# A hybrid decoder layer on one core: inputs handed over a second time with channels on rows, and the first pair of heads issued earlier

## The chip, the core and the metric

The kernel runs on one core of a Trainium2 chip. The metric is device time in microseconds (us) of one execution, as the median of several runs. A core has five engines with instruction queues of their own: TensorE (PE, matmuls; its weight loads are shown apart as PEld), VectorE (DVE), ScalarE (ACT), GpSimd (POOL) and SyncE (SP), which issues most of the transfers here. SP's transfers and POOL's transfers are moved by the same 16 DMA engines.

## What is computed

The input `x` has 256 tokens of 2048 channels, in fp32. The layer is a SwiGLU block of width 5632, a mixer, a second SwiGLU block, and a last norm:

```
x = x + 0.5 * (silu(n1(x) @ w1) * (n1(x) @ w3)) @ w2          # ffn1
h = rms_norm(x, mix_norm);  p = h @ w_in                      # q|k, v, o, gates, u
y = [ mLSTM heads (4 heads, causal, 64-token chunks) | S5 (64 groups, complex diagonal scan) ] @ w_out
x = x + y
x = x + 0.5 * swiglu_2(rms_norm(x));   out = rms_norm(x, final_norm)
```

In a head the 256x256 scores of q and k are multiplied by a decay matrix and then multiplied with v. In S5, each group has a state of 64 complex numbers; its output is the real part of the states times `c_re + i c_im`.

## The kernel before

**Precision by three products.** Each fp32 operand is split in two parts (`xh`, `xl` and `whi`, `wlo`), and a product is `xh*whi + xl*whi + xh*wlo`. A weight step is 256 rows by 512 columns (512 KB): SP loads it into `wraw` (L155), ACT casts it to `whi` (L157), DVE subtracts to get `wlo` (L159), and PE runs 12 matmuls of 128x512 (`step_tok`, L177). There are four buffers each of `wraw`, `whi` and `wlo`, and `weights` keeps up to three further steps in preparation (`AHEAD`).

**The activations need channels on rows.** `x` comes with tokens on rows. `transpose_x` (L341) turns a chunk of 512 channels with 8 PE transposes, ACT writes `xh` times the norm's gain (L346), DVE writes `xl` (L351). The gains are themselves loaded as rows and turned by PE (`vec0` at L272 and `vecs` at L294).

**The opening** is the function `start`: the first product of ffn1 (8 steps), in an order written out by hand for PE, ACT and DVE. It loads x chunk by chunk, transposes a chunk after steps 0, 2 and 4, runs `self.warm` (matmuls on a zero tile, L312) before the data is there, and takes the squares for the norm (`sumsq`) in steps 4 to 7. SP's order is written out by hand in the whole kernel. Elsewhere the order on PE, ACT, DVE and POOL is set when the kernel is built, out of program order and readiness; each engine then takes its instructions one after the other.

**Hooks and background tasks.** `self.after(n, f)` runs `f` after n further weight steps; `self.bg` is a list of small tasks of which `tick` issues a few after each step (the S5 parameters during ffn1, and the S5 scan of eight groups `j` during the mixer: load, drive, scan, unrotate, emit, act). For each `j`, `per_j` builds the S5 matrices; its `stage_c` and `trans` spread C over two parities of groups with a mask (DVE), turn it with two PE transposes (L734) and copy it out of PSUM (ACT L735, L736).

**The mixer around the change.** The products come in the order u, o, q|k, v, then `w_out`. The v product has two halves `c` of 8 steps each, here called v0 and v1. Its result is moved out by ACT into `vx[c]` (L1040). During v1 the hooks run: `scores(0)` after step 1, `scores(1)` after 2, `heads(0)` after 4, `scores(2)` after 5, `scores(3)` after 6, `heads_T(0)` after 7. `scores(h)` is four PE matmuls (L964, L965) and one DVE instruction that writes `Dm` (L966). `heads(0)` is 12 PE matmuls that read `Dm` of heads 0 and 1 and `vx[0]`, and take all four banks of the PSUM pool `tp` (L991, L994); ACT and DVE evacuate them. `heads_T(0)` turns the result (L1024), ACT writes `hmh` (L1029), DVE writes `hml` (L1030), and the first `w_out` product reads both. On the DVE queue between them stand the weights' subtractions, the S5 scan (L867) and the S5 output `yT` (L894); on ACT's stand the weights' casts and the S5 activation (L898), which reads `yT`.

Of the kernel before, what the change touches and what calls it, by code (L numbers as in the profile page):

```python
# [8 lines left out]
F32 = mybir.dt.float32  # L9
# [7 lines left out]
P = 128  # L17
S = 256
# [22 lines left out]
WARM = 8  # L41
MORE_WARM = 4
# [20 lines left out]
class _Layer:  # L63
# [87 lines left out]
    def fetch(self, name, k, kk, c0, n):  # L151
        nc = self.nc
        view = self.wview(name)
        raw = self.wraw.tile([P, KK * NC], F32, name="wraw")[:, :kk * n]
        nc.sync.dma_start(out=raw.rearrange("p (k n) -> p k n", n=n), in_=view[:, k:k + kk, c0:c0 + n])  # L155
        hi = self.whi.tile([P, KK * NC], F32R, name="whi")[:, :kk * n]
        nc.scalar.copy(hi, raw)  # L157
        lo = self.wlo.tile([P, KK * NC], F32R, name="wlo")[:, :kk * n]
        nc.vector.tensor_sub(lo, raw, hi.bitcast(F32))  # L159
        return hi.rearrange("p (k n) -> p k n", n=n), lo.rearrange("p (k n) -> p k n", n=n)  # L160
# [28 lines left out]
    def start(self, acc, view, gain):  # L189

        W = lambda i: self.weights(view, i * KK, KK, 0, NC)
        M = lambda i, w: self.step_tok(acc, self.xs, [(i * KK, 0), (i * KK + 1, 0)], w, NC, i == 0, i == 7)
        T = lambda c, halves=(0, 1): self.transpose_x(c, gain, halves)
# [44 lines left out]
    def setup(self):  # L238
# [16 lines left out]
        vec0 = self.s5p.tile([KD, P], F32, name="vec0", tag="s5k0")  # L255
        nc.sync.dma_start(out=vec0, in_=self.a["ffn1_norm"][0].rearrange("(k p) -> k p", p=P))
# [13 lines left out]
        self.cols0 = c.tile([P, KD], F32, name="cols0")  # L270
        b = self.bank()
        nc.tensor.transpose(b[:, :KD], vec0, self.ident[:KD, :KD])  # L272
        nc.vector.tensor_copy(self.cols0, b[:, :KD])
        rows = 16 + 16 + 32 + 8 * 4
        vecs = self.s5p.tile([rows, P], F32, name="vecs", tag="s5k0")
        r = 0
        where = {}
        for name, n in (("mix_norm", 16), ("ffn2_norm", 16), ("conv_w", 32), ("conv_b", 8), ("mlstm_norm", 8),
                        ("d_skip", 8), ("b_glu", 8)):
            src = self.a[name][0]  # L280
            if name == "conv_w":
                src = src.rearrange("w (j p) -> (w j) p", p=P)
            elif name == "d_skip":
                src = src.rearrange("(j r) h -> j (r h)", r=8)
            else:
                src = src.rearrange("(k p) -> k p", p=P)
            nc.gpsimd.dma_start(out=vecs[r:r + n, :], in_=src)
            where[name] = r
            r += n
        self.cols = c.tile([P, rows], F32, name="cols")  # L290

        def late():
            b = self.bank()
            nc.tensor.transpose(b[:, :rows], vecs, self.ident[:rows, :rows])  # L294
            nc.vector.tensor_copy(self.cols, b[:, :rows])
            w = where["b_glu"]
            nc.vector.tensor_scalar(self.cols[:, w:w + 8], self.cols[:, w:w + 8], 0.5, None, op0=ALU.mult)
            w = where["mlstm_norm"]
            nc.vector.tensor_scalar(self.cols[:, w:w + 8], self.cols[:, w:w + 8], 0.5, None, op0=ALU.mult)
# [3 lines left out]
        nc.vector.memset(self.gcol, 0.0)  # L303
        for i, name in enumerate(("b_i", "b_f")):
            nc.gpsimd.dma_start(out=self.gcol[32 * i:32 * i + H, :], in_=self.a[name][0].rearrange("(h o) -> h o", o=1))
# [62 lines left out]
    def ffn(self, l, chunk_done):  # L368
        nc = self.nc
        w1, w3, w2 = (f"ffn{l}_{n}" for n in ("w1", "w3", "w2"))  # L370
        with ExitStack() as ctx:
# [4 lines left out]
            for hi_, n in enumerate(HALVES):  # L376
                gs = []
                self.rate = self.ffn1_rate if l == 1 else 1
                for c in range(n):
                    cc = c0 + c  # L380
                    ks = [(k, k) for k in range(KD)]
                    p1 = self.pair()
                    if l == 1 and cc == 0:
                        self.start(p1, w1, lambda k: self.cols0[:, k:k + 1])
                    else:
                        self.gemm_tok(p1, self.xs, w1, ks, cc * NC, NC)
                    s = []
                    for t in range(TT):
                        s.append(fp.tile([P, NC], F32, name=f"s{t}"))
                        nc.scalar.activation(s[t], p1[t], AF.Silu, scale=self.rstd[:, t:t + 1])  # L390
# [117 lines left out]
    def s5_params(self, ctx):  # L508
# [13 lines left out]
        craw = [sp.tile([P, NJ, 64], F32, name=f"craw{i}") for i in range(2)]  # L522
# [14 lines left out]
        for i, nm in enumerate(("c_re", "c_im")):  # L537
            load(out=craw[i], in_=self.a[nm][0].rearrange("(j r) h p -> (r h) j p", r=8))
# [4 lines left out]
        maskg = sp.tile([P, 2], F32, name="maskg")  # L543
        maskq = sp.tile([P, 4], F32, name="maskq")

        def layout():
# [11 lines left out]
            V.tensor_reduce(maskg, self.ident.rearrange("p (q g h) -> p g q h", q=4, g=2), op=ALU.add, axis=AX.XY)  # L558
# [130 lines left out]
        def per_j(j):  # L689
# [26 lines left out]
            stc = [st.tile([P, 2, 64], F32, name=f"stc{ri}") for ri in range(2)]  # L716
# [61 lines left out]
    def mixer(self, chunk_done):  # L778
# [4 lines left out]
        with ExitStack() as ctx:  # L783
# [453 lines left out]
```

## Time and profile before

| what | value |
|---|---|
| time, median of 3 runs | 1839.52 us (1839.28 to 1840.48) |
| the profiled execution: its own time | 1839.91 us |
| its span, first to last instruction | 1838.2 us |
| mean granted TensorE clock | 0.996 |
| busy: PE, DVE, ACT, POOL | 99%, 58%, 45%, 19% |
| transfers | 358.26 MB, mean 195 GB/s |

The profiled execution's time is its span and 1.7 us around it. Busy is the time in which an engine had an instruction running; matmuls are pipelined and their ends are modelled, so PE's 99% says that it had almost always something to do, not that it ran at its peak. An "idle" in brackets behind a row is the time for which the engine had nothing to do before it, and the instruction that ended this.

### The profile page before, as it was taken

To read this page: it belongs to the slowest core of one execution; us is meant where nothing else is said; L and a number is where in the kernel's file an instruction comes from. 1 tells how busy PE (TensorE), PEld (TensorE's weight loads), DVE (VectorE), ACT (ScalarE), POOL (GpSimd) and SP (SyncE) were. 2 spreads that over 40 slices of the span, in tenths; PEclk is the share of its full clock that TensorE was granted. 3 is DMA by queue.
4 is the path that set the end of the run, shared out by engine and by line. 5 is a ranking of instruction groups with operands and counts; after the bars stand their busy time and mean duration, and the time that the engine had idled before them with its cause. 6 is when DMAs were issued, how large, how long until landed. Compare 5 with 4: busy or idle time off the path is not lost.

```text
span 1838.2 us, 24018 instructions
## 1 busy us (share of the span) xinstructions
PE 1821.5 (99%) x9174; PEld 1527.0 (83%) x9174; DVE 1064.4 (58%) x1261; ACT 818.1 (45%) x982; POOL 348.9 (19%) x519
## 2 busy tenths in 40 slices
PE   9999999999999999999999999999999999999998
PEld 7888888888888888998977988888888888888887
DVE  5546855555555555578888665454544545454554
ACT  6444444334444445444454564444443334444343
POOL 4000799920000000065545100000000000000011
PEclk9999999999999999999999999999999999999999
DMA  8666676676666665767784556666665666666563
GB/s 275 196 186 185 192 217 214 213 242 196 196 197 195 188 198 195 198 181 208 184 211 149 190 189 201 193 192 189 189 187 192 193 194 191 189 193 186 193 193 128
DMA packets 185652, 358.26 MB, mean 195 GB/s; under 512 B 12064, under 2 KB 18336, under 8 KB 185408
## 3 DMA queue, kind: packets, MB, share of 16 engines
q1 hardware_dynamic: 181344, 344.51, 63.1%
q0 software_dynamic: 4048, 11.16, 1.7%
q8 instruction: 72, 1.18, 0.3%
q10 hardware_dynamic: 144, 1.05, 0.1%
q14 instruction: 44, 0.36, 0.1%
HBM read 344.61 MB, written 11.01 MB: 193 GB/s over the span
## 4 chain that ended last, share of the span: by engine, by line
PE 95%; DVE 2%; DMA 2%; issue 1%; ACT 0%; ACTq 0%; POOLq 0%; POOL 0%; SPq 0%; DVEq 0%
PE accb L177 84%; PE accb L225 2%; PE accb L231 2%; PE accb L226 2%; DVE wlo L159 1%; PE tpb L492 1%; DMA wraw<-in_w_in_dram 1%; PE tpb L341 0%; DMA wraw<-in_ffn_w_dram 0%; PE tpb L852 0%; PE accb L482 0%; PE accb L481 0%; PE accb L480 0%; PE tpb L891 0%; PE tpb L928 0%
## 5 line engine op out<-in xcount | busy, mean ns | idle before, releaser
L159 DVE TENSOR_TENSOR wlo<-wraw,whi 128x1024 fp32r<-128x1024 f32 x622 | 791.1, 1274 | 677.4 <-ACT whi L157 676.8
L157 ACT CAST whi<-wraw 128x1024 fp32r<-128x1024 f32 x622 | 654.4, 1053 | 885.3 <-PE accb L177 814.4
L177 PE MATMUL accb<-whi,xh 128*128 128x512 f32 x1536 | 603.5, 393 | 0.6 <-ACT whi L157 0.6
L177 PE MATMUL accb<-whi,xl 128*128 128x512 f32 x1536 | 598.9, 390 | 0.8 <-DVE xl L351 0.8
L177 PE MATMUL accb<-wlo,xh 128*128 128x512 f32 x1536 | 410.7, 389 | 0.0
L177 PEld LDWEIGHTS accb<-whi,xh 128*128 128x128 f32 x1536 | 289.0, 188 | 61.6 <-ACT whi L157 1.3
L177 PEld LDWEIGHTS accb<-whi,xl 128*128 128x128 f32 x1536 | 289.0, 188 | 60.3 <-DVE xl L351 1.6
L177 PEld LDWEIGHTS accb<-wlo,xh 128*128 128x128 f32 x1536 | 288.3, 188 | 60.1
L177 PE MATMUL accb<-whi,gh 128*128 128x512 f32 x664 | 259.8, 391 | 0.0
L177 PE MATMUL accb<-whi,gl 128*128 128x512 f32 x664 | 258.4, 389 | 0.0
L177 PE MATMUL accb<-wlo,gh 128*128 128x512 f32 x664 | 177.5, 389 | 0.0
L177 PEld LDWEIGHTS accb<-wlo,gh 128*128 128x128 f32 x664 | 124.6, 188 | 25.9
L177 PEld LDWEIGHTS accb<-whi,gh 128*128 128x128 f32 x664 | 124.6, 188 | 25.6
L177 PEld LDWEIGHTS accb<-whi,gl 128*128 128x128 f32 x664 | 124.7, 188 | 25.5
L1201 POOL TENSOR_TENSOR x<-x,fn 128x512 f32<-128x512 f32 x6 | 12.1, 2041 | 689.9 <-ACT junk L323 689.9
L703 POOL TENSOR_TENSOR tr<-s5rot,sp 128x128 f32<-128x128 f32 (+6 forms) x112 | 55.5, 496 | 160.2 <-DVE sp L643 156.7
L225 PE MATMUL accb<-xh,whi 128*128 128x256 f32 x256 | 63.5, 286 | 0.0
L226 PE MATMUL accb<-xl,whi 128*128 128x256 f32 x256 | 62.8, 283 | 0.0
L705 POOL TENSOR_TENSOR s5rot<-tr,tr 128x128 f32<-128x128 f32 (+6 forms) x112 | 61.0, 557 | 3.3
L704 POOL TENSOR_TENSOR tr<-s5rot,sp 128x128 f32<-128x128 f32 (+6 forms) x112 | 57.2, 511 | 0.0
L764 POOL DMA_DIRECT2D spillw<-s5w x16 | 8.6, 541 | 249.6 <-ACT s5w L735 239.2
L225 PEld LDWEIGHTS accb<-xh,whi 128*128 128x128 f32 x256 | 49.1, 192 | 0.8 <-issue 0.4
(316 smaller groups left out, 1345.5 us busy)
## 6 DMA issues: line engine op xcount, KB each, us to landing
wraw<-in_ffn_w_dram SPq DMA_DIRECT2D x528, 512.0 KB, 3.8
wraw<-in_w_in_dram SPq DMA_DIRECT2D x64, 512.0 KB, 5.7
wraw<-in_w_out_dram SPq DMA_DIRECT2D x32, 512.0 KB, 4.2
spillrot<-s5rot POOLq DMA_DIRECT2D x8, 512.0 KB, 5.4
spillw<-s5w POOLq DMA_DIRECT2D x16, 256.0 KB, 4.6
s5rot<-spillrot SPq DMA_DIRECT2D x8, 512.0 KB, 6.9
s5w<-spillw SPq DMA_DIRECT2D x16, 256.0 KB, 7.1
wraw<-in_w_glu_dram SPq DMA_DIRECT2D x8, 512.0 KB, 3.7
```

The source lines that it names most:

```text
L157: nc.scalar.copy(hi, raw)
L159: nc.vector.tensor_sub(lo, raw, hi.bitcast(F32))
L177: nc.tensor.matmul(acc[t][:, :n], lhsT=x, rhs=wt, start=first and t not in seen, stop=last and t not in left)
L225: nc.tensor.matmul(o(nt), lhsT=wh[:, kk, ns(nt)], rhs=xh, start=st, stop=False, **kw)
L226: nc.tensor.matmul(o(nt), lhsT=wh[:, kk, ns(nt)], rhs=xl, start=False, stop=False, **kw)
L231: nc.tensor.matmul(o(nt), lhsT=wl[:, kk, ns(nt)], rhs=xh, start=False, stop=sp, **kw)
L492: nc.tensor.transpose(b[:, o:o + P], s[t][:, kt * P:(kt + 1) * P], self.ident)
L703: G.tensor_tensor(tr[0][:, :, :k], rv[:, 0, :, 0:k], u0, op=ALU.mult)
L704: G.tensor_tensor(tr[1][:, :, :k], rv[:, 1, :, 0:k], u1, op=ALU.mult)
L705: G.tensor_tensor(rv[:, a, :, k:2 * k], tr[0][:, :, :k], tr[1][:, :, :k], op=op)
L764: nc.gpsimd.dma_start(out=d, in_=t)
L1201: nc.gpsimd.tensor_tensor(self.x[c][:, t, :], self.x[c][:, t, :], self.fn[:, c * NC:(c + 1) * NC], op=ALU.mult)
```

## The change

It has four parts.

1. **x with channels on rows.** A copy of x with channels on rows (`xT`) is handed over beside x. In the opening SP loads `xT` in place of x (the first chunk in two halves, the first weight step in two halves too); ACT and DVE write `xh` and `xl` from it, and the PE transposes of the opening go. Splits of x and of weights are written two steps ahead of the matmuls. x itself is still wanted for the norm and the sum: it is loaded in steps 4 to 7, its squares are taken in steps 1 to 4 of the next product (`w3`), and `finish_rstd` and the silu of the first product follow there. The zero-tile matmuls are 9 in place of 8 and 4. The raw `xT` lies in the `gl` buffers, which are free then.
2. **Channel vectors** come as one array `cols`, loaded first by SP (57 KB in rows of 448 bytes); two PE transposes, their copies, seven loads on POOL's queue and one on SP's go. The gate biases are one load on POOL's queue in place of two.
3. **S5's C** is handed over turned and spread (`cT`). Per `j`, two loads of 64 KB on POOL's queue write it into the tile `w2`; two PE transposes, two DVE products and two ACT copies go, and one ACT instruction, which changes the sign of the imaginary part in place, is added. Two loads of C on POOL's queue before that (256 KB each) go.
4. **Order in the v product.** `scores(0)` and `scores(1)` run after steps 6 and 7 of v0, `heads(0)` after step 2 of v1, `scores(2)` and `scores(3)` after steps 4 and 5, `heads_T(0)` after step 6.

```diff
-WARM = 8
-MORE_WARM = 4
+WARM = 9
...
         with self.tc.manual_schedule(engines={ET.PE, ET.Activation, ET.DVE}):
-            self.load_x(0)
-            T(0, (0,))
-            self.ahead.append((self.steps[0], self.fetch(*self.steps.pop(0))))
-            T(0, (1,))
-            self.warm(MORE_WARM)
-            self.ahead.append((self.steps[0], self.fetch(*self.steps.pop(0))))
-            self.load_x(1)
+            load_xT(0, 0, 2)
+            load(0, KK)
+            load_xT(0, 2, 4)
+            load(1)
+            prepare(0)
+            load_xT(1)
+            load(2)
+            prepare(1)
+            load_xT(2)
+            load(3)
             for i in range(8):
-                M(i, W(i))
-                if i % 2 == 0 and i < 6:
-                    T(i // 2 + 1)
-                if i % 2 == 0 and i < 4:
-                    self.load_x(i // 2 + 2)
+                prepare(i + 2)
+                if i == 0:
+                    load_xT(3)
+                if i + 4 < 10:
+                    load(i + 4)
                 if i >= 4:
-                    self.sumsq(i - 4)
-        self.finish_rstd()
+                    self.load_x(i - 4)
+                self.step_tok(acc, self.xs, [(i * KK, 0), (i * KK + 1, 0)], ready.pop(0)[1], NC, i == 0, i == 7)
+        self.ahead = ready
...
+        def split_x(k):
+            c, i = divmod(k, 4)
+            g = self.col("ffn1_norm", k)
+            nc.scalar.activation(self.xh[c][:, i, :], raw[c][:, i, :], AF.Copy, scale=g)
+            nc.vector.scalar_tensor_tensor(self.xl[c][:, i, :], raw[c][:, i, :], g, self.xh[c][:, i, :].bitcast(F32),
+                                           op0=ALU.mult, op1=ALU.subtract)
...
                     if l == 1 and cc == 0:
-                        self.start(p1, w1, lambda k: self.cols0[:, k:k + 1])
+                        self.start(p1, gp)
+                        for i in range(4):
+                            self.after(1 + i, lambda i=i: self.sumsq(i))
+                        self.after(4, self.finish_rstd)
+                        self.after(4, silu)
...
             def stage_c():
                 for ri in range(2):
-                    src = craw[ri][:, j, :].unsqueeze(1).broadcast_to([P, 2, 64])
-                    self.tc.keep_in_program_order(V.tensor_tensor(
-                        stc[ri], src, maskg.unsqueeze(2).broadcast_to([P, 2, 64]), op=ALU.mult))
+                    nc.gpsimd.dma_start(out=w2[:, ri * P:(ri + 1) * P], in_=self.a["cT"][ri, :, j, :])
...
-                b2 = self.bank()
-                for ri in range(2):
-                    nc.tensor.transpose(b2[:, ri * P:(ri + 1) * P], stc[ri].rearrange("p g q -> p (g q)"), self.ident)
-                nc.scalar.copy(w2[:, 0:128], b2[:, 0:128])
-                nc.scalar.activation(w2[:, 128:256], b2[:, 128:256], AF.Copy, scale=-1.0)
+                nc.scalar.activation(w2[:, 128:256], w2[:, 128:256], AF.Copy, scale=-1.0)
...
+                if c == 0:
+                    self.after(6, lambda: scores(0))
+                    self.after(7, lambda: scores(1))
                 acc = self.pair()
                 self.gemm_tok(acc, self.xs, win, ks, V0 + c * NC, NC)
...
                 if c == 0:
-                    for h, n in enumerate((1, 2, 5, 6)):
-                        self.after(n, lambda h=h: scores(h))
-                    self.after(4, lambda: heads(0))
-                    self.after(7, lambda: heads_T(0))
+                    self.after(2, lambda: heads(0))
+                    self.after(4, lambda: scores(2))
+                    self.after(5, lambda: scores(3))
+                    self.after(6, lambda: heads_T(0))
```

## Rows read from the trace of the kernel before

**Rows 1.** The page, part 1: busy us, share of the span, instructions, by engine.

```profile
PE 1821.5 (99%) x9174; PEld 1527.0 (83%) x9174; DVE 1064.4 (58%) x1261; ACT 818.1 (45%) x982; POOL 348.9 (19%) x519
```

**Rows 2.** Chain that ended last, around the opening: start us, us, what.

```profile
25.75 0.87 PE tpb L341 x8
26.62 24.50 PE accb L177 x108
```

**Rows 3.** Timeline of PE, opening: start us, us, line, out<-in, [idle before <-releaser].

```profile
1.52 3.59 PE L312 MATMUL tpb<-junk 128*128 128x512 bf16 x8 [1.52 <-DVE junk L260]
5.97 1.09 PE L341 MATMUL tpb<-ident,x 128*128 128x128 f32 x8 [0.69 <-DMA x<-in_x_dram]
8.49 0.50 PE L177 MATMUL accb<-whi,xh 128*128 128x512 f32 x1 [0.57 <-ACT whi L157]
...
34.63 0.39 PE L177 MATMUL accb<-whi,xh 128*128 128x512 f32 x1
```

**Rows 4.** Windows of the opening: busy us by engine, PEclk, DMA share, GB/s last.

```profile
8.50:12.50 4.00, 4.00 (x22) 3.41 (x23) 3.16 (x5) 2.67 (x4) 3.54 (x5) 1.00 1.06 402
12.50:17.50 5.00, 4.96 (x22) 3.79 (x21) 3.98 (x6) 2.52 (x5) 0.00 (x0) 1.00 1.06 264
```

**Rows 5.** Timeline, opening: POOL's first load in small pieces; ACT's third weight cast.

```profile
8.39 1.22 POOL L526 DMA_DIRECT2D wgr<-in_w_in_dram  x1 [1.51 <-DMA vecs<-in_ffn_norm_dram]
...
11.38 1.04 ACT L157 CAST whi<-wraw 128x1024 fp32r<-128x1024 f32 x1 [1.26 <-DMA wraw<-in_ffn_w_dram]
```

**Rows 6.** Groups by line on ACT, first 60 us: count, busy us, mean ns.

```profile
L346 ACT ACTIVATE xh<-tpb,cols 128x256 fp32r<-128x256 f32 x16 | 6.4, 474 | 4.6 <-PE tpb L341 4.6
```

**Rows 7.** Loads: queue, count, KB each, median us from issue to landing.

```profile
vec<-in_ffn_norm_dram SPq DMA_DIRECT2D x1, 8.0 KB, 1.6
...
vecs<-in_conv_b_dram POOLq DMA_DIRECT2D x1, 4.0 KB, 5.8
```

**Rows 8.** Chain that ended last, around one `trans` of ffn1.

```profile
241.43 13.62 PE accb L177 x60
255.70 19.08 PE accb L177 x84
```

**Rows 9.** Timeline of PE in v1 and at the start of `w_out`.

```profile
940.62 0.59 PE L964 MATMUL tpb<-qkc 128*128 128x256 f32 x2
...
952.92 1.10 PE L991 MATMUL tpb<-vx,Dm 128*128 128x257 f32 x4 [2.57 <-DVE Dm L966]
...
968.64 1.03 PE L1024 MATMUL tpb<-ident,oth 128*128 128x128 f32 x8
...
973.57 0.50 PE L177 MATMUL accb<-whi,hmh 128*128 128x512 f32 x1
976.29 0.50 PE L177 MATMUL accb<-whi,hml 128*128 128x512 f32 x1 [2.22 <-DVE hml L1030]
```

**Rows 10.** Windows of 20 us around v1 and `w_out`; PEclk is third from last.

```profile
940.00:960.00 20.00, 17.43 (x72) 13.71 (x70) 15.51 (x14) 8.61 (x16) 10.99 (x6) 0.91 0.81 226
960.00:980.00 20.00, 17.54 (x115) 13.92 (x115) 17.12 (x31) 9.16 (x18) 11.60 (x7) 0.95 0.39 122
980.00:1000.00 20.00, 20.00 (x97) 15.74 (x96) 14.67 (x29) 11.88 (x25) 4.16 (x4) 0.97 0.55 186
```

**Rows 11.** Timeline of DVE in the same stretch.

```profile
940.59 4.46 DVE L159 TENSOR_TENSOR wlo<-wraw,whi 128x1024 fp32r<-128x1024 f32 x2
944.98 0.47 DVE L894 SCALAR_TENSOR_TENSOR yT<-uT,cols,tpb 128x256 f32<-128x256 f32 x1
...
970.28 3.42 DVE L867 TENSOR_TENSOR_SCAN A<-Rt,A 128x512 f32<-128x512 f32 x2 [0.71 <-POOL A L860]
...
975.76 0.87 DVE L1030 SCALAR_TENSOR_TENSOR hml<-tpb,cols,hmh 128x256 fp32r<-128x256 f32 x2
```

**Rows 12.** Timeline of ACT in the same stretch.

```profile
945.48 0.42 ACT L898 ACTIVATE yT<-yT 128x256 f32<-128x256 f32 x1 [6.70 <-DVE yT L894]
...
946.74 1.26 ACT L1040 ACTIVATE vx<-accb,rstd 128x512 f32<-128x512 f32 x2
```

More of the change, by code (lines that the diff above doesn't have):

```diff
@@ L149, in weights, with fetch, load, split_tiles @@
         return w
-    def fetch(self, name, k, kk, c0, n):
-        nc = self.nc
[L153 to L160, printed above, removed]
+    def fetch(self, *step):
+        return self.split(self.load(*step))
+    def load(self, name, k, kk, c0, n, parts=1):
+        raw = self.wraw.tile([P, KK * NC], F32, name="wraw")[:, :kk * n].rearrange("p (k n) -> p k n", n=n)
+        m = kk // parts
+        for i in range(0, kk, m):
+            self.nc.sync.dma_start(out=raw[:, i:i + m, :], in_=self.wview(name)[:, k + i:k + i + m, c0:c0 + n])
+        return raw
+    def split_tiles(self):
+        return (self.whi.tile([P, KK * NC], F32R, name="whi"), self.wlo.tile([P, KK * NC], F32R, name="wlo"))
+    def split(self, raw, tiles=None, ks=None):
+        nc = self.nc
+        kk, n = raw.shape[1:]
+        hi, lo = (t[:, :kk * n].rearrange("p (k n) -> p k n", n=n) for t in tiles or self.split_tiles())
+        ks = ks or slice(0, kk)
+        nc.scalar.copy(hi[:, ks, :], raw[:, ks, :])
+        nc.vector.tensor_sub(lo[:, ks, :], raw[:, ks, :], hi[:, ks, :].bitcast(F32))
+        return hi, lo
     def step_tok(self, acc, xs, part, w, n, first, last):
@@ L254, in setup @@
         xin = self.a["x"][0].rearrange("(t p) n -> p t n", p=P)
-        vec0 = self.s5p.tile([KD, P], F32, name="vec0", tag="s5k0")
-        nc.sync.dma_start(out=vec0, in_=self.a["ffn1_norm"][0].rearrange("(k p) -> k p", p=P))
+        rows = sum(n for _, n in _COLS)
+        self.cols = c.tile([P, rows], F32, name="cols")
+        nc.sync.dma_start(out=self.cols, in_=self.a["cols"])
         self.load_x = lambda i, a=0, b=NC: nc.sync.dma_start(out=self.x[i][:, :, a:b],
@@ L269, in setup @@
         nc.vector.memset(self.mhalf, -0.5)
[L270 to L287, printed above, removed]
+        where, r = {}, 0
+        for name, n in _COLS:
             where[name] = r
             r += n
-        self.cols = c.tile([P, rows], F32, name="cols")
         def late():
[L293 to L299, printed above, removed]
+            for name in ("b_glu", "mlstm_norm"):
+                w = where[name]
+                nc.vector.tensor_scalar(self.cols[:, w:w + 8], self.cols[:, w:w + 8], 0.5, None, op0=ALU.mult)
         self.after(6, late)
@@ L302, in setup @@
         self.gcol = c.tile([GW, 1], F32, name="gcol")
-        nc.vector.memset(self.gcol, 0.0)
-        for i, name in enumerate(("b_i", "b_f")):
-            nc.gpsimd.dma_start(out=self.gcol[32 * i:32 * i + H, :], in_=self.a[name][0].rearrange("(h o) -> h o", o=1))
+        nc.gpsimd.dma_start(out=self.gcol, in_=self.a["gcol"])
         self.wgr = c.tile([P, KD, 2 * H], F32, name="wgr")
@@ L382, in ffn, with silu @@
                     p1 = self.pair()
-                    if l == 1 and cc == 0:
-                        self.start(p1, w1, lambda k: self.cols0[:, k:k + 1])
+                    s = []
+                    def silu(p1=p1, s=s):
+                        for t in range(TT):
+                            s.append(fp.tile([P, NC], F32, name=f"s{t}"))
+                            nc.scalar.activation(s[t], p1[t], AF.Silu, scale=self.rstd[:, t:t + 1])
+                    if l == 1 and cc == 0:
+                        self.start(p1, gp)
[3 more added lines that the diff above has]
+                        self.after(4, silu)
                     else:
                         self.gemm_tok(p1, self.xs, w1, ks, cc * NC, NC)
[L387 to L390, printed above, removed]
+                        silu()
                     p3 = self.pair()
@@ L1216, with _layout @@
 _OUT = (1, S, D)
+def _layout(inputs):
+    import numpy as _np
+    a = {name: inputs[name] for name in _INS}
+    f = lambda name: _np.asarray(inputs[name][0])
+    cols = lambda v: v.reshape(-1, P).T
+    a["xT"] = f("x").T.reshape(KD, P, S).transpose(1, 0, 2)
+    a["cols"] = _np.concatenate([cols(f(name)) for name, _ in _COLS], axis=1)
+    gcol = _np.zeros((GW, 1), _np.float32)
+    gcol[0:H, 0], gcol[32:32 + H, 0] = f("b_i"), f("b_f")
+    a["gcol"] = gcol
+    cT = _np.zeros((2, 2, 64, NJ, 8, 16), _np.float32)
+    for i, name in enumerate(("c_re", "c_im")):
+        c = f(name).reshape(NJ, 8, 16, 64).transpose(3, 0, 1, 2)
+        for g in range(2):
+            cT[i, g, :, :, g::2] = c[:, :, g::2]
+    a["cT"] = cT.reshape(2, P, NJ, P)
+    return a
 def kernel(**inputs):
@@ L1227 @@
     arrays, args = {}, {}
-    for name in _INS:
-        v = _np.ascontiguousarray(inputs[name])
+    for name, v in _layout(inputs).items():
+        v = _np.ascontiguousarray(v)
         arrays[f"in_{name}_dram"] = v
```

36 lines of the change are left out of this document (26 added, 10 removed).

## The prediction

> **What bounds the kernel now.** I read the page's first part, then the chain that ended last, then the timelines where the chain leaves PE. PE is busy for 1821.5 of 1838.2 us [rows 1], and long stretches of the chain are matmuls in a row: 108 of them take 24.50 us [rows 2], so one costs 0.227 us and a weight step of 12 costs 2.72 us. Nothing in this change makes a step cheaper. It can win only where PE does something other than these steps or stands still, and there are three such places. In the opening the first step starts at 8.49 us and the next product (`w3`) at 34.63 us [rows 3]; eight steps need 21.8 us, so 26.1 - 21.8 = 4.3 us of that stretch are transposes and waits, beside the late start. In ffn1 PE turns S5's C. In the mixer PE stands idle for 2.57 us before `heads(0)` and for 2.22 us at the first `hml` matmul [rows 9]. [...]
>
> **The opening.** Before, the first x chunk (0.52 MB, with a vector ahead) was there at 5.97 us [rows 3]. After, the first split needs `cols` and half a chunk, 0.32 MB: 0.2 MB less, which at 402 to 264 GB/s [rows 4] is 0.5 to 0.8 us less, so 5.3 us. The halves of the first weight step make 0.58 and 0.84 MB: about 6.1 and 6.9 us. ACT then takes them in turn: `xh` 0.47 us [rows 6], a half cast 0.52 us (half of 1.04 [rows 5]), and again: the casts end at about 6.65 and 7.7 us. Eight matmuls are left then (1.8 us), so step 0 ends near 9.5 us. Seven steps of 2.72 us bring `w3` to 28.6 us if no load is late. It gains 6.0 us over 34.63, of which 2.6 us are the three groups of eight transposes at 0.87 us [rows 2].
>
> A load can be late. Through step 4 SP brings 4.8 MB in the order of need; before, the third weight step (2.6 MB in) landed at 11.38 us [rows 5], and at 402 GB/s the fifth would land near 16.6 us, with a cast ready about when PE wants it (9.5 + 3 x 2.72 = 17.7 us). There is no slack, and one thing eats into it: POOL's loads of small pieces (`wgr`, then S5's B) started at 8.39 us, behind eight others on POOL's queue [rows 5], and once they ran the rate fell from 402 to 264 GB/s for 5 us [rows 4]. After the change only one load stands ahead of them, so they come some 5 us earlier, inside the stretch where nothing may be late. The loss is (402 - 264) x 5 us = 0.69 MB, 1.7 us at 402 GB/s, and I charge all of it: **the opening gains 4.3 us**. Bounds: 6.0 us where it charges nothing; 2.0 us where `cols` lands as late as the slowest small load (5.8 us after issue, not 1.6 [rows 7]; that moves step 0 by 0.6 us) and the clock falls as behind the mixer's idle times (1.7 us), for the zero matmuls end near 1.52 + 9 x 0.45 = 5.6 us [rows 3] and PE is idle from there to 6.7 us. I take neither: that idle time is half of the shorter one that was followed by a fall.
>
> [...]
>
> The second copy of x (2.1 MB) goes out behind the weights of steps 8 and 9 and is wanted only for squares; PE takes 193 GB/s of weights (512 KB in 2.72 us), so half the rate is free for it. The squares, `rstd` and silu, moved behind it, are covered by the eight steps of `w3`: their first reader on PE's path is the transposition after `w3`. Without this cover a late silu would hold PE for as long as it is late. All other vector loads are off the path.
>
> **S5's C and the vectors.** Around one `trans` PE goes from 255.05 (241.43 + 13.62) to 255.70 us [rows 8]: 0.65 us for six transposes, 0.109 each. Sixteen go, with one for the vectors on the path: 17 x 0.109 = **1.85 us**. In exchange ACT waits for a load on POOL's queue that is issued two tasks earlier. Behind that wait stand ACT's weight casts, and PE would wait for them; three prepared steps, 8.2 us, cover it, and in ffn1 POOL stood waiting for ACT, not ACT for POOL. I cost it at nothing (bounds 0 and one loss of 1.85).
>
> **The order in the v product.** `heads(0)` needs `Dm` and `vx[0]`. Before, PE reached it at 952.92 - 2.57 = 950.35 us. Two steps earlier that is 944.9 us. `Dm` moves along: its scores come three steps earlier, and DVE's write of 0.5 us can stand ahead of the scan. But `vx[0]` doesn't: ACT wrote it at 946.74 to 948.0, directly behind a stand of 6.70 us for `yT` [rows 12], and `yT` came at 944.98 behind two subtractions that took 2.2 us each beside POOL's work [rows 11]. Nothing in the change moves `yT`, and ACT's order there isn't written by hand. So **the wait changes its cause**: PE waits for `vx[0]` from 944.9 to 948.0, 3.1 us in place of 2.57, the clock falls as before, and this place **loses 0.5 us** (bounds: loses 1.0 if `yT` slips behind a `Dm`, gains 4.3 if ACT writes `vx[0]` first).
>
> Then the second idle time. Before, `heads_T(0)` was on PE at 968.64 us, DVE turned to the scan at 970.28 (3.42 us) and a subtraction, and wrote `hml` only at 975.76, while PE was at `w_out` from 973.57 [rows 9, 11]. The scan itself had waited for POOL until 970.28. One step earlier, `hml` is ready to be written some 2.7 us sooner, near 967.5, when the scan can't run yet: it goes ahead, and `w_out`, now two steps behind, finds it. **That returns 2.22 + 1.7 = 3.9 us.** Bounds: 0 and 3.9. Next in line is `heads(1)`, which waits for nothing before.
>
> **Sum**: 4.3 + 1.85 - 0.5 + 3.9 = 9.55 us from the profiled execution's 1839.91 us gives 1830.4; the median is 0.4 us below that execution, so 1830.0 us.
>
> **The rivals.**
> - *Both idle times go* (ACT writes `vx[0]` ahead of the S5 activation). For: `vx[0]`'s matmuls are done long before ACT gets to it. Against: the S5 emission keeps its place in the order of tasks, and `heads(0)` takes all four banks, so `scores(2)` waits for DVE's evacuation. 4.3 + 1.85 + 4.3 + 3.9 = 14.35: 1825.2 us.
> - *The second idle time stays*: DVE keeps the scan ahead of `hml`. For: DVE was busy for 17.1 of 20 us from 960 us [rows 10], and the order on it isn't in the diff. 4.3 + 1.85 - 0.5 = 5.65: 1833.9 us. That the earlier hooks don't do what they say ends here too.
> - *The opening returns nothing*: POOL's pieces hold up the first operands. With this and the second idle time kept, 1.85 - 0.5: 1838.2 us.
> - *Slower: the opening starves.* If POOL's pieces and the double x hold the rate at half of 402 GB/s through the opening, the 6.35 MB through step 7 take some 32 us from 2.5 us on, `w3` starts at 34.5 + 1.1 + 2.7 = 38.3, 3.7 us later than before, and PE, idle before each step, takes two falls of the clock (3.4 us): 1839.5 + 3.7 + 3.4 - 1.35 = 1845.3 us. It decides as soon as `w3` starts later than 36 us. Against: 264 GB/s lasted 5 us only.
>
> **How the numbers follow.** My forecast 0.45, both go 0.2, the second stays 0.22, nothing from the opening 0.06, starved 0.07. The range reaches from the second case with the opening's upper bound (1825.2 - 1.7 = 1823.5) to the third with the opening's lower bound (1833.9 + 2.3 = 1836.2). A measurement of this kernel tells 0.2%, 3.7 us, from no change: below 1835.8 is faster. The third case's late part and the fourth fill the middle: faster 0.85, same 0.09, slower 0.06.
>
> **What would show it.** Right: `w3`'s first matmul near 30.3 us, no L341 before it; DMA rate low between 6 and 12 us; a wait of PE at L991 for ACT's `vx`, about 3 us; `hml` on DVE ahead of the scan and no wait at `w_out`; no L734; a mean clock near 0.998. Wrong: `w3` past 32 us, a clock of 0.5 behind the zero matmuls, casts of ACT in ffn1 waiting for POOL's loads of C, or a wait of PE for `scores(2)`'s bank.

## The result and the profile after

The changed kernel takes 1901.39 us (median of 4 runs, 1899.89 to 1901.66) against 1839.57 us of the kernel before beside it: a ratio of 1.033, interval 1.032 to 1.035. It is 3.3% slower where I had forecast 0.5% faster. The profiled execution took 1901.13 us. Line numbers in this section are those of the changed kernel; under the experiments they are those of each run's own kernel.

The page's first part, against [rows 1]:

```profile
span 1899.4 us, 23911 instructions
...
PE 1819.5 (96%) x9121; PEld 1523.1 (80%) x9121; DVE 1054.0 (55%) x1242; ACT 817.7 (43%) x975; POOL 322.0 (17%) x525
```

PE is busy for 2.0 us less than before and the span is 61.2 us longer, so PE got no more work: it stands still. What it waited for is in the view of PE's waits (releaser: us in total, times, longest):

```profile
PE accb L187 <- DVE wlo L169: 57.9, 2, 57.4
PE accb L187 <- ACT whi L168: 7.4, 4, 4.4
PE tpb L1008 <- ACT vx L1060: 3.1, 1, 3.1
PE tpb L335 <- DVE junk L306: 1.5, 1, 1.5
PE accb L187 <- ACT hmh L1046: 1.3, 1, 1.3
PE accb L187 <- DVE hml L1047: 0.3, 1, 0.3
```

One wait of 57.4 us is nearly the whole result. The start of the same work in both traces shows where the 61 us arise (us; in brackets the difference from before):

| kernel | first `split_T` | 6th `split_T` | gate matmuls, start of the mixer | ffn2's first `split_T` | last matmul |
|---|---|---|---|---|---|
| before | 61.98 | 286.01 | 778.30 | 1149.49 | 1829.90 |
| after | 65.09 (+3.1) | 349.52 (+63.5) | 840.63 (+62.3) | 1210.20 (+60.7) | 1890.98 (+61.1) |

(`split_T` turns the product of `w1` and `w3` for `w2`; the first one ends the opening and the steps of `w3`.) So up to there 3.1 us were lost where I had the opening gain 4.3; ffn1 lost 59 us (the 5th `split_T`, at 243.6 us, was still 3.2 us behind); the mixer returned 1.6 us.

**The loss in ffn1**, in the timelines of ACT, DVE, PE and POOL (start, duration, engine, line, operation; in brackets the idle time before and its releaser):

```profile
338.89 0.31 ACT L753 ACTIVATE s5w<-s5w 128x128 f32<-128x128 f32 x1 [65.88 <-DMA s5w<-in_cT_dram]
...
338.70 0.29 DVE L760 TENSOR_TENSOR tw<-s5w,sp 128x128 f32<-128x128 f32 x1 [66.25 <-DMA s5w<-in_cT_dram]
...
340.19 2.07 PE L187 MATMUL accb<-wlo,xh 128*128 128x512 f32 x4 [57.39 <-DVE wlo L169]
...
25.96 1.10 POOL L743 DMA_DIRECT2D s5w<-in_cT_dram  x2
27.12 1.07 POOL L743 DMA_DIRECT2D s5w<-in_cT_dram  x2
...
279.65 0.54 POOL L781 DMA_DIRECT2D spillw<-s5w  x1
...
335.60 1.09 POOL L743 DMA_DIRECT2D s5w<-in_cT_dram  x2
```

ACT came to the sign change of C's part `j` = 2 at 338.89 - 65.88 = 273.0 us, and DVE to the first product of `clam` (which multiplies C by the S5 factors) at 272.5 us. Both read the tile that the load of C fills. That load was issued at 335.60 us. POOL had loaded parts 0 and 1 at 26 and 27 us, when both buffers of the tile were new; the third load had to wait until part 0 was written back (`spillw`, from 279.65 us on) and for its own turn behind the S5 tables on POOL's queue. So the weight casts and subtractions stood 66 us on both engines, PE used up the prepared steps until 282.8 us and then stood 57.4 us. The windows show PE's busy time, the clock (third number from the end) and the rate (last), while POOL worked on:

```profile
250.00:300.00 50.00, 32.79 (x159) 26.58 (x157) 11.97 (x13) 10.34 (x11) 47.56 (x137) 0.85 0.42 137
300.00:350.00 50.00, 9.81 (x33) 7.85 (x34) 9.29 (x14) 5.72 (x7) 34.84 (x107) 0.54 0.27 91
```

After the wait the first 16 matmuls, from 340.19 to 346.80 us, took 6.61 us, where 16 x 0.227 [rows 2] are 3.6, so 3.0 us more; the granted clock of that stretch is 0.54.

**The opening**, against [rows 3, 5]: POOL's small loads, then PE and ACT.

```profile
2.50 1.23 POOL L555 DMA_DIRECT2D wgr<-in_w_in_dram  x1
...
6.20 0.50 PE L187 MATMUL accb<-whi,xh 128*128 128x512 f32 x1 [0.86 <-ACT whi L168]
...
12.59 1.04 ACT L168 CAST whi<-wraw 128x1024 fp32r<-128x1024 f32 x1 [4.10 <-DMA wraw<-in_ffn_w_dram]
...
13.68 0.80 PE L187 MATMUL accb<-whi,xh 128*128 128x512 f32 x1 [4.44 <-ACT whi L168]
```

The first matmul comes 2.3 us sooner than in [rows 3], but the second weight step lands only near 12.5 us. The windows point to the cause: the rate against [rows 4].

```profile
5.00:7.50 2.50, 1.64 (x8) 1.04 (x7) 1.80 (x4) 1.73 (x4) 1.19 (x2) 1.00 1.14 368
7.50:11.50 4.00, 1.74 (x8) 1.10 (x7) 1.45 (x4) 0.91 (x2) 0.00 (x0) 1.00 0.96 226
...
12.50:17.50 5.00, 3.82 (x9) 3.04 (x10) 2.42 (x5) 3.14 (x5) 2.65 (x3) 0.50 1.05 371
```

The dip that was harmless at 12.5 to 17.5 us before comes at 7.5 to 11.5 us now, and PE works at a granted clock of 0.50 (12.5 to 17.5 us) behind its wait. `w3` starts at 35.19 us, against 34.63 before and 30.3 in the forecast. So only 0.6 of the 3.1 us are lost ahead of `w3`; the other 2.5 arise in its steps (PE, then ACT):

```profile
35.19 0.39 PE L187 MATMUL accb<-whi,xh 128*128 128x512 f32 x1
42.40 0.50 PE L187 MATMUL accb<-whi,xh 128*128 128x512 f32 x1 [1.60 <-ACT whi L168]
...
41.32 1.03 ACT L168 CAST whi<-wraw 128x1024 fp32r<-128x1024 f32 x1
```

ACT took six of the moved squares in a row, from 36.91 us on, and only then this cast.

**The mixer**, against [rows 9 to 12]:

```profile
1010.20 1.14 PE L1008 MATMUL tpb<-vx,Dm 128*128 128x257 f32 x4 [3.09 <-ACT vx L1060]
...
1008.21 0.42 ACT L915 ACTIVATE yT<-yT 128x256 f32<-128x256 f32 x1 [6.71 <-DVE yT L911]
...
1009.47 1.26 ACT L1060 ACTIVATE vx<-accb,rstd 128x512 f32<-128x512 f32 x2
...
1029.16 0.87 DVE L1047 SCALAR_TENSOR_TENSOR hml<-tpb,cols,hmh 128x256 fp32r<-128x256 f32 x2
1030.43 2.31 DVE L884 TENSOR_TENSOR_SCAN A<-Rt,A 128x512 f32<-128x512 f32 x1 [0.40 <-POOL A L877]
1032.66 0.84 DVE L1047 SCALAR_TENSOR_TENSOR hml<-tpb,cols,hmh 128x256 fp32r<-128x256 f32 x2
...
1051.63 0.73 PE L187 MATMUL accb<-whi,hmh 128*128 128x512 f32 x2 [1.29 <-ACT hmh L1046]
...
1053.10 1.22 PE L187 MATMUL accb<-whi,hml 128*128 128x512 f32 x2 [0.32 <-DVE hml L1047]
```

`heads(0)` waits 3.09 us for `vx[0]`, which stands behind the S5 activation; two of the four `hml` instructions are ahead of the scan and two between its halves, and `w_out` (from 1034.20 us) starts without a wait. The waits are as forecast. New is a pair of waits at 1051.63 and 1053.10 us, behind the second pair's `heads_T`.

### The profile page after: what moved, and what is told of

Its sections match the earlier page's. It is cut to its first block, busy times and chain, and to the rows that moved or that the text cites. A ratio compares the mean times of both kernels' runs of the same rounds, so it can differ in the third digit from the quotient of the medians.

```text
span 1899.4 us, 23911 instructions
## 1 busy us (share of the span) xinstructions
PE 1819.5 (96%) x9121; PEld 1523.1 (80%) x9121; DVE 1054.0 (55%) x1242; ACT 817.7 (43%) x975; POOL 322.0 (17%) x525
## 3 DMA queue, kind: packets, MB, share of 16 engines
q1 hardware_dynamic: 182192, 346.66, 61.1%
## 4 chain that ended last, share of the span: by engine, by line
PE 86%; POOL 7%; DVE 3%; issue 1%; ACT 1%; DMA 1%; SPq 0%; POOLq 0%; ACTq 0%; DVEq 0%
PE accb L187 75%; POOL tr L728 2%; POOL s5rot L730 2%; POOL tr L729 2%; PE accb L270 2%; PE accb L276 2%; PE accb L271 2%; DVE wlo L169 2%; PE tpb L522 1%; DMA wraw<-in_ffn_w_dram 0%; ACT whi L168 0%; PE tpb L869 0%; PE accb L512 0%; PE accb L511 0%; PE accb L510 0%
## 5 line engine op out<-in xcount | busy, mean ns | idle before, releaser
L169 DVE TENSOR_TENSOR wlo<-wraw,whi 128x1024 fp32r<-128x1024 f32 (+1 forms) x623 | 787.4, 1267 | 674.7 <-ACT whi L168 672.9
L168 ACT CAST whi<-wraw 128x1024 fp32r<-128x1024 f32 (+1 forms) x623 | 653.8, 1051 | 871.2 <-PE accb L187 792.6
L728 POOL TENSOR_TENSOR tr<-s5rot,sp 128x4 f32<-128x4 f32 (+6 forms) x112 | 50.6, 452 | 146.9 <-DVE sp L668 143.8
L271 PEld LDWEIGHTS accb<-xl,whi 128*128 128x128 f32 x256 | 49.1, 192 | 0.1
L730 POOL TENSOR_TENSOR s5rot<-tr,tr 128x4 f32<-128x4 f32 (+6 forms) x112 | 47.3, 435 | 3.0
```

Of the source, the lines that this page charges most:

```text
L168: nc.scalar.copy(hi[:, ks, :], raw[:, ks, :])
L169: nc.vector.tensor_sub(lo[:, ks, :], raw[:, ks, :], hi[:, ks, :].bitcast(F32))
L271: nc.tensor.matmul(o(nt), lhsT=wh[:, kk, ns(nt)], rhs=xl, start=False, stop=False, **kw)
L728: G.tensor_tensor(tr[0][:, :, :k], rv[:, 0, :, 0:k], u0, op=ALU.mult)
L730: G.tensor_tensor(rv[:, a, :, k:2 * k], tr[0][:, :, :k], tr[1][:, :, :k], op=op)
```

## Experiments

In all of them the reference's whole computation is done. "First `split_T`" is that of the table, and "part" is one of the eight groups `j` of C. The same opening differs by some 1 us between two traces: the first `split_T` is at 61.98 us in the kernel before and at 60.95 us in run 4, which has the same opening.

**1. C transposed as before, the rest changed.** `stage_c` and `trans` are those of the kernel before, and so are POOL's two loads of C at the start.

```diff
-                    nc.gpsimd.dma_start(out=w2[:, ri * P:(ri + 1) * P], in_=self.a["cT"][ri, :, j, :])
+                    self.tc.keep_in_program_order(V.tensor_tensor(stc[ri], src, maskg..., op=ALU.mult))
...
+                    nc.tensor.transpose(b2[:, ri * P:(ri + 1) * P], stc[ri]..., self.ident)
+                nc.scalar.copy(w2[:, 0:128], b2[:, 0:128])
```

> The changed kernel with C made as before: both halves of C loaded once by POOL at the start, masked by VectorE, transposed by TensorE (16 transposes of 109 ns more, 1.75 us). Everything else of the change stays. Theory Q (the loss is C's load, which stands on POOL's queue behind POOL's own tables): the wait of 57.4 us at 340 us in TensorE's row goes, with the 1.7 us at a low clock behind it, so 1901.4 - 59.1 = 1842.3 us, between 1840.5 and 1844; the first split_T keeps its +3.1 us. Rival N (something else that the change moved, the x load by rows or the order of the first steps, starves ffn1): the time stays above 1890.

Measured: 1842.58 us (1839.78 to 1844.51), ratio 1.0017, interval 1.0008 to 1.0026. The 6th `split_T` is at 288.95 us, 2.9 us behind before, as the first one is. So the 59 us are C's alone (rival N falls), and x and the vectors by rows lose some 3 us up to there. Its opening is that of the changed kernel, but the wait falls a step later: 3.28 us, ahead of the third step, at 17.20 us.

**2. C loaded whole and early.**

```diff
+        for i in range(2):
+            load(out=ct[:, i], in_=self.a["cT"][i])
...
+                nc.scalar.copy(w2[:, 0:128], ct[:, 0, j, :])
+                nc.scalar.activation(w2[:, 128:256], ct[:, 1, j, :], AF.Copy, scale=-1.0)
```

> The changed kernel, but C with channels on rows is loaded whole into one tile of its own (8 KB a partition) among the first loads of POOL, and ScalarE copies each part from there into the S5 tile, one copy more for each of the 8 parts. No transposes of C on TensorE. Theory Q: no wait of 57 us, and 16 transposes of 109 ns fewer than in the run with C transposed: 1842.3 - 1.75 = 1840.5 us, between 1838.5 and 1842.5. Rival N: above 1890. If the transposes were hidden beside other work after all, the time equals that of the run with C transposed within 0.5 us.

Measured: 1850.40 us (1847.22 to 1855.69), 10 us above theory Q. No wait for a load of C was left, and yet ACT stood in the same place, now for the S5 tile to be written back:

```profile
290.39 0.30 ACT L755 COPY s5w<-ct 128x128 f32<-128x128 f32 x1 [10.07 <-DMA spillw<-s5w]
```

ACT came to the copy for part 2 at 280.3 us; the `trans` that it belongs to comes far later (ACT is at it from 386.65 us on in the kernel before). Theory Q doesn't say why ACT wanted part 2 so early. The opening lost more as well (first `split_T` 67.47).

**3. Eight small tiles for C, loaded where the change loads them.**

```diff
-                    nc.gpsimd.dma_start(out=w2[:, ri * P:(ri + 1) * P], in_=self.a["cT"][ri, :, j, :])
+                    nc.gpsimd.dma_start(out=ct[j][:, ri, :], in_=self.a["cT"][ri, :, j, :])
```

> C's load stays where the change has it, on POOL's queue at its place in each part's steps, but it goes into one of 8 small tiles of its own, so it waits for no S5 buffer to be written back; ScalarE copies it into the S5 tile. Theory Q (queue order behind POOL's tables decides): part 2's load is still issued only when the tables of part 1 are done, near 335 us, and the wait near 340 us stays at 50 to 60 us: 1895 to 1903 us. Rival B (the release of the S5 buffer, of which there are two, decides): the wait goes, 1840 to 1843 us.

Measured: 1851.36 us (one run, so its spread isn't known), 44 us below theory Q's range and 8 above rival B's. But the run doesn't tell Q from B as I meant: with nothing to wait for, all 16 loads moved into the opening (27 to 36 us), and none was left behind the tables. The first `split_T` fell back to 72.02, and ACT stood 13.03 us for `spillw` at 289.73.

**4. The order in the v product alone, in the kernel before** (part 4 of the diff, nothing else).

> The kernel before with nothing but the order of the first pair's scores and heads moved, as the change has it. If the 1.6 us that the mixer gave back in the changed kernel is a property of this order alone: 1838.0 us, between 1836.5 and 1839.5, with a wait of about 3.1 us at the heads' first matmul that names vx and none of 2.2 us before the output product. My forecast's terms for it (0.5 lost, 3.9 returned) give 1836.2. The rival, that the wait at the heads only changes its cause and the other idle place only moves, gives the time before within 0.5 us.

Measured: 1836.90 us (1835.65 to 1838.21) against 1839.29, ratio 0.9987, interval 0.9978 to 0.9996: 2.4 us gained. The wait at the heads is 3.13 us and names `vx`; before `w_out` there is none; 0.74 and 0.32 us stand behind the second pair's `heads_T`. The interval is 1835.2 to 1838.6 us: it holds the forecast's terms (1836.2) and the smaller gain of the trace (1838.0), so it doesn't decide between them; the rival, the time before within 0.5 us, lies outside.

**5. ACT's sign change held in its step.** Runs 2 and 3 gave a new theory: before, the transposes held all that reads C in its place, and without them these instructions float ahead in their engines' order.

```diff
-                nc.scalar.activation(w2[:, 128:256], w2[:, 128:256], AF.Copy, scale=-1.0)
+                self.tc.keep_in_program_order(nc.scalar.activation(
+                    w2[:, 128:256], w2[:, 128:256], AF.Copy, scale=-1.0))
```

> The changed kernel with one thing more: ScalarE's negation of C's second half is held behind the instruction that the source puts ahead of it (the copy of w1 in the same trans step), as the transposes held it before the change. C's loads stay on POOL's queue, into the S5 tile. Theory F (the negation has lost what tied it to its step and floated ahead in ScalarE's order, to 273 us for part 2, while its step comes near 386 us, by when C has long landed): the wait of 57 us is gone, 1842.6 (the run with C transposed) less 16 transposes of 109 ns = 1840.8 us, between 1839 and 1843. Rival Q (POOL's queue delivers C too late for its step wherever the negation stands): a wait of 8 us or more stays, 1849 us or more.

Measured: 1900.27 us (1898.46 to 1900.50). Nothing came back. The timeline shows that ACT's instruction had left and DVE's stood there still; ACT's casts then waited for the weights behind it:

```profile
337.96 0.29 DVE L761 TENSOR_TENSOR tw<-s5w,sp 128x128 f32<-128x128 f32 x1 [67.08 <-DMA s5w<-in_cT_dram]
...
343.40 1.05 ACT L168 CAST whi<-wraw 128x1024 fp32r<-128x1024 f32 x1 [63.87 <-DMA wraw<-in_ffn_w_dram]
```

**6. Both held.** In addition DVE's first product of `clam`:

```diff
-                V.tensor_tensor(tw[0], w[:, 0], lr_, op=ALU.mult)
+                self.tc.keep_in_program_order(V.tensor_tensor(tw[0], w[:, 0], lr_, op=ALU.mult))
```

> As the run with ScalarE's negation held in its step, and VectorE's first product that reads C (the first line of clam) held in its step too. With the negation alone held, VectorE stood 67 us at that product, for the same load, and the weights behind it. Theory F2 (every instruction that reads C straight from its load has lost the transposes that tied it to its step; the first of them on each engine floats ahead and blocks that engine): the wait at 340 us is gone, 1900.3 - 58.3 of wait - some 1.7 of low clock = 1840.3 us, between 1838.5 and 1843. Rival Q (the load on POOL's queue is too late for its step wherever its readers stand): 1849 us or more.

Measured: 1839.14 us (1837.73 to 1841.82), ratio 1.0000, interval 0.9991 to 1.0009. Two lines return the 62 us by which the changed kernel is slower.

```profile
370.66 1.09 POOL L743 DMA_DIRECT2D s5w<-in_cT_dram  x2 [5.97 <-PE accb L187]
...
385.03 0.32 ACT L753 ACTIVATE s5w<-s5w 128x128 f32<-128x128 f32 x1
...
386.21 0.28 DVE L762 TENSOR_TENSOR tw<-s5w,sp 128x128 f32<-128x128 f32 x1
```

C's load for part 2 is still on POOL's queue behind the tables, at 370.66 us even later than in the changed kernel (335.60); its readers come 14 us after it and wait for nothing. So POOL's queue set how long the wait was, and the place of the readers made it a wait (rival Q falls).

**7. POOL's loads held back until x is split**, in run 1's kernel, in run 2's with the copies held, and in the kernel before. A one-element copy on POOL from the last quarter of `xl` into each tile precedes its load:

```diff
-            tasks.append(lambda: nc.gpsimd.dma_start(**kw))
+            def go():
+                o = kw["out"]
+                src = self.xl[3][0:1, 0:1, 0:1] if len(o.shape) == 3 else self.xl[3][0:1, 0, 0:1]
+                nc.gpsimd.tensor_copy(o[tuple(slice(0, 1) for _ in o.shape)], src.bitcast(F32))
+                nc.gpsimd.dma_start(**kw)
+            tasks.append(go)
```

> The changed kernel with C transposed as before, and POOL's loads (w_in's gate columns in 32-byte pieces, the S5 parameters, C) made to wait until the last quarter of x is split, by one POOL element copy each. Theory O (in the opening POOL's small loads, which now start at 2.5 us and no longer at 8.4 us, halve the DMA rate just when x's second quarter and w1's third step are to come): the wait of 3.3 us before the third step and the clock's fall behind it go, w3's first matmul comes near 30 us, 1842.6 - 5 = 1837.6 us, between 1835.5 and 1839.5. Rival S (x in two layouts, 4 MB in place of 2, and the smaller first loads on SP's queue set the opening): 1841.5 us or more.

> C with channels on rows loaded whole into a tile of its own, ScalarE's two copies of each part held in their step, and POOL's loads (w_in's gate columns, the S5 parameters, C) made to wait until the last quarter of x is split, by one POOL element copy each into the tile they fill. Theory F says no wait for C, theory O (POOL's small loads take DMA rate from x and w1 in the opening) says that the opening is back: the run with only the loads gated less 16 transposes of 109 ns, 1835.8 us, between 1834 and 1838. If the transposes of C were hidden: equal to that run within 0.5 us. If neither holds: above 1840.

> The kernel before with POOL's loads of w_in's gate columns and of the S5 parameters gated in the same way, nothing else. Theory O: its opening waited for transposes and casts more than for loads (waits of 0.6 to 0.8 us), so it gains little: 1838.5 us, between 1837 and 1839.5. If gating helps any opening as much as the changed one: 1834 to 1836 us.

Measured: 1847.83, 1845.09 and 1844.86 us, all slower than expected, the first and the last slower than without the gate (1842.58 and 1839.42). In the first of them PE ran without a break from 6.73 to 38.4 us, and then stood 12.07 us. The gate had put fourteen loads ahead of `rstd` on POOL's queue:

```profile
29.81 0.94 POOL L560 DMA_DIRECT2D braw<-in_b_re_dram  x1
36.98 2.64 POOL L560 DMA_DIRECT2D braw<-in_b_re_dram  x3 [6.23 <-issue]
...
47.45 0.75 POOL L387 TENSOR_TENSOR rstd<-ms,mhalf 128x2 f32<-128x2 f32 x1
...
48.24 1.27 ACT L411 ACTIVATE s<-accb,rstd 128x512 f32<-128x512 f32 x2 [13.04 <-POOL rstd L387]
...
50.49 0.80 PE L187 MATMUL accb<-whi,xh 128*128 128x512 f32 x1 [12.07 <-ACT whi L168]
```

So the gate did for the opening what theory O says and cost more elsewhere.

**8. The same gate, behind `rstd`**, in run 1's kernel and in the kernel before; the copy reads `self.rstd`.

> As the gated run with C transposed, but POOL's loads wait for the rows' scale (rstd, which POOL itself computes near 42 us) in place of x's last quarter. With the first gate TensorE ran without a break from 6.7 to 38.4 us and then stood 12.1 us, since rstd was on POOL's queue behind the loads that had been held back (ScalarE waited 13.0 us for it). Theory O: the opening's gain stays and that wait goes: its first split_T at 71.4 - 12.1 - about 2.7 of low clock = 56.6 us against 64.8 in the run with C transposed, so 1842.6 - 8.2 = 1834.4 us, between 1832.5 and 1837. Rival S (x in two layouts or the rest of the order costs what is lost): 1841 us or more.

> The kernel before with POOL's loads of w_in's gate columns and of the S5 parameters made to wait for rstd, nothing else. From its run with the first gate: first split_T at 67.3 - 3.8 of wait - about 2.7 of low clock = 60.8 us against 62.0, so 1838.2 us, between 1836.5 and 1839.6: the old opening is bound by its transposes and casts and gains little. If the gain is the gate's on any opening: 1834 us or less.

Measured: 1833.84 us (1832.32 to 1835.67), ratio 0.9970, interval 0.9958 to 0.9981; and 1839.14 us, ratio 0.9997, interval 0.9988 to 1.0006. The changed opening now ends 4.3 us ahead of before (first `split_T` 57.65) and run 1 without the gate ended 2.9 behind; the old one gains 1.4 us in its trace and nothing that its times can tell. So POOL's early loads are what the new opening lost by (rival S falls), and it is the new order that is sensitive to them. The gate holds all of them, C's two loads too; that the ones in small pieces do the harm is read from the rate and wasn't tried by itself.

**9. All together**: C early in a tile of its own, its two copies held in their step, POOL's loads behind `rstd`.

> The changed kernel with C loaded whole into a tile of its own, ScalarE's two copies of it held in their step, and POOL's loads made to wait for rstd. Theories F2 and O together: the run with the loads gated late and C transposed, less 16 transposes of 109 ns: 1832.6 us, between 1830.5 and 1835. If the transposes of C were hidden beside other work: equal to that run within 0.5 us.

Measured: 1831.39 us (1830.39 to 1832.02) against 1839.17, ratio 0.9956, interval 0.9943 to 0.9970: it beats both kernels. PE's waits in it:

```profile
PE tpb L1016 <- ACT vx L1068: 3.1, 1, 3.1
PE tpb L335 <- DVE junk L306: 1.5, 1, 1.5
PE accb L187 <- ACT whi L168: 0.7, 1, 0.7
PE accb L187 <- ACT hmh L1054: 0.7, 1, 0.7
PE accb L187 <- DVE hml L1055: 0.3, 1, 0.3
```

One window of the opening shows the difference to the changed kernel best: PE is busy for 6.00 of 6 us and the rate is 406 GB/s, where the changed kernel (second line) had 1.56 us and 291 GB/s.

```profile
8.00:14.00 6.00, 6.00 (x22) 4.74 (x22) 4.78 (x10) 3.94 (x7) 0.00 (x0) 1.00 1.03 406
...
8.00:14.00 6.00, 1.56 (x7) 1.00 (x6) 1.42 (x4) 1.53 (x3) 0.86 (x1) 0.82 0.95 291
```

The first line's clock column says 1.00, but the first step took 4.96 us (6.29 to 11.25) for 12 matmuls without a wait between them, where a step takes 2.72; what slowed that step isn't shown. `w3` starts at 30.30 us here and at 29.50 us in run 8's changed opening.

## Why the prediction was wrong, point by point

**S5's C: the failed step.** The prediction set ACT's wait for a load on POOL's queue at nothing, since "three prepared steps, 8.2 us, cover it, and in ffn1 POOL stood waiting for ACT, not ACT for POOL". The cover was about right in size: PE went on for 9.8 us after ACT stood still (273.0 to 282.8) and was back 1.3 us after ACT, so 65.88 - 9.8 + 1.3 = 57.4 us of standing were left. Wrong was the wait that it had to cover. I took the place of C's readers in ACT's and DVE's order as given. It was given by the instructions that the change removes: in the kernel before `stage_c`'s product is held in program order, and the transposes and copies depend on it. Afterwards ACT's and DVE's readers depend on the load alone, and in the order that is fixed ahead of the run they moved to where the load was expected: ACT's came at 32 and 34 us for parts 0 and 1 and at 273 us for part 2, against 385 us where its step is (run 6). POOL issued the load 62.6 us after that. That the readers moved, and that with both held in their step the wait is gone, is shown (runs 5 and 6); that the order went by a time for POOL's tables that was too short is argued from it. The trace of before could have warned: POOL is busy for 47.77 of the 50 us from 250 us on and for 48.07 of the next 50, and part 0 is written back only behind that:

```profile
374.11 1.08 POOL L764 DMA_DIRECT2D spillw<-s5w  x2
```

That POOL waits for ACT was true of the later parts, when the tables were done. Nor was DVE in the prediction: run 5 shows that its product alone costs the same. My list of signs had the casts of ACT waiting for loads of C as what would prove me wrong, but none of the rivals had a price for it.

The gain from fewer transposes is there: run 9 against the first of run 8 gives 2.45 us, and in the traces 1.4 us of it by the gate matmuls (772.74 against 774.09); sixteen of them were 1.74 of my 1.85. Every execution of run 9 (up to 1832.02) is below every one of run 8 (from 1832.32), so there is a gain; but the intervals of the two ratios overlap, and its size isn't settled.

**The opening: right in its parts, wrong in one size and one cover.** The first step came at 6.20 us, near what I had worked out. I charged POOL's small loads 1.7 us (and counted eight loads ahead of them on POOL's queue before, where the trace has nine). With them in place PE had the wait of 4.44 us at the second step, and slow matmuls from 13.68 to 18.83 us, 5.15 us for a step of 2.72 at a granted clock of 0.52, so `w3` came 4.9 us later than forecast. The price went by the bytes not moved; but the bytes that were late were those of the next step, and the clock's fall nearly doubled the next step. I also wrote that the squares of x are covered by the eight steps of `w3`. They weren't quite: ACT's squares, then its silu, stood ahead of casts, and PE waited 1.60 us at 42.40 and 0.46 at 45.91. With POOL's loads held back one wait of 0.51 us (run 8) or none (run 9) is left there. There the first `split_T` gains 4.3 us (57.65 against 61.98), which is my term to the tenth, by luck: the 4.3 included 1.7 for loads that are out of the way there, and at `w3` run 8 is 5.1 us ahead (29.50). In times, run 1 against run 4, whose kernels differ in x and the vectors alone, is 5.7 us lost (in their traces 3.9 of it up to the first `split_T`, most of the rest in the mixer); run 8 against run 4 is 3.1 us gained.

While POOL's small loads were among SP's, from 7.5 to 11.5 us, the 16 DMA engines were busy for 0.96 of the time and moved 226 GB/s, after 368 in the 2.5 us before. To issue C's loads early didn't help by itself: runs 2 and 3 made the opening worse by 2.6 and 7.2 us than run 1's. In run 6 they are issued late, and the readers, held in their step 14 us behind the load, wait for nothing.

**The mixer: right in mechanism, too large.** The wait for `vx[0]` is 3.09 us, as worked out; `hml` no longer stands behind the whole scan; `w_out` starts without a wait. The forecast of 3.4 us left out what is late next. I wrote that `heads(1)` waits for nothing before; it doesn't now either, but its `heads_T(1)` comes 1.3 + 0.3 us too late for `w_out`'s second half, and the clock falls once, there (0.91) or at the heads (0.91 in run 4). So 3.1 + 1.6 of waiting and one fall (1.8 us: 0.09 of 20 us) stand in place of 8.2 (2.57 + 2.22 of waiting [rows 9], and the (0.09 + 0.05 + 0.03) x 20 = 3.4 us by which the three windows of [rows 10] are short of a clock of 1.00): 1.7 us returned, 1.6 in the trace of after, and 2.4 in the times of run 4, where the second pair's waits are 1.1 us. No run shows the fixed 1.7 us that the forecast takes for a fall of the clock, in the mixer, in the opening's lower bound and twice in the starving rival; it was my estimate, half of those 3.4 us, and the 1.7 us of low clock in what I expected of runs 1 and 6 are the same figure. The runs showed some 1.8 us in run 4, 2.4 in the changed opening (5.15 - 2.72), 3.0 behind the wait of 57.4 us, and some 3.4 in run 6.

**The rivals.** The slower one was priced at 1845.3 us for a starving opening. Its mechanism was there in part (run 1: 1842.58), but its size is not the result's. None had the wait of 57 us.

## What to carry to other kernels

An instruction that is taken out also takes its dependences with it: ask for each one that stays what still holds it in its place, and on which engine it would block when the order fixed ahead of the run has it where its operand isn't there yet. Here a load on a compute engine's queue was issued only when that engine's earlier work was done (335.60 us), so a stretch in which that engine is busy without a gap is the number to look up before a wait on it is set at nothing. When loads go from a queue, ask which of those behind them move forward, and what they meet there. Here POOL's early loads cost nothing that the times can tell in the kernel before (small pieces from 8.39 us on [rows 5]; 1839.14 us with the loads held back, 1839.17 without) and 8.7 us in the changed one with C transposed (from 2.50 us on in the changed kernel; run 8's 1833.84 us against run 1's 1842.58).

## What the runs showed of the hardware

The same idle time did or did not bring the clock down. In the changed kernel PE stood 3.09 us at the heads and the 20 us around it were at 1.00; in run 4 it stood 3.13 us, and they were at 0.91. Where the clock held, the next wait, 1.29 us behind the second `heads_T`, was followed by a fall (0.91, second line); in run 4 that wait was 0.74 us and the clock held. So one fall was paid either way. The first kernel of run 8 went on like the changed kernel (3.07 us and 1.00 over the 20 us around them; then 1.3 us and 0.91), runs 6 and 9 like run 4 (3.1 us each, 0.83 and 0.91 over 20 us; then 0.6 and 0.7 us, and 1.00). What a fall costs differs too: some 1.8 us in run 4 (a granted clock of 0.91 over 20 us), some 3.4 in run 6 (0.83 over the 20 us from 940 us on). The windows of the changed kernel, then of run 4:

```profile
1000.00:1020.00 20.00, 16.91 (x77) 13.82 (x76) 17.02 (x27) 9.81 (x20) 13.08 (x8) 1.00 0.85 195
...
1040.00:1060.00 20.00, 18.25 (x82) 13.65 (x81) 14.16 (x28) 10.22 (x22) 5.65 (x4) 0.91 0.54 186
```

```profile
936.00:956.00 20.00, 16.87 (x68) 13.53 (x67) 17.05 (x25) 10.20 (x19) 13.57 (x9) 0.91 0.83 208
...
976.00:996.00 20.00, 18.94 (x94) 14.75 (x93) 14.90 (x29) 11.56 (x25) 6.26 (x5) 1.00 0.59 205
```

What decides whether the clock falls, and for how long, wasn't tried. The second surprise is POOL's issue of loads in small pieces: between the first two of its eight loads of S5's B, POOL did nothing else for 6.23 us (run 7, marked "issue"; 6.24 in the kernel before, 6.95 in the changed one). So from the first of them to the second far more of POOL's time went by than the 0.9 us of the first one's own row; what it waits for there isn't shown.
